# A 3x3 convolution by Winograd rows: the first image pair is loaded in two pieces, one of them ahead of the weights

## The chip, the cores and the metric

The kernel runs on one core of one Trainium2 chip. The metric is the device time of one execution in microseconds, lower is better. Before the change it is 126.67 us, the median of three runs (126.33 to 126.72).

A core has five engines that run side by side and wait for one another by semaphores: TensorE (PE) for matrix products, VectorE (DVE), ScalarE (ACT) and GpSimd (POOL) for elementwise work, and SyncE (SP), which here only issues transfers. Transfers between the chip's main memory and the core's own memory run on 16 DMA engines, which serve the queues of SyncE, ScalarE and GpSimd together.

## The reference

Sixteen images of 64 channels and 64 x 64 pixels are convolved with 128 filters of 64 x 3 x 3, with a border of one zero pixel. All is float32.

```python
x_pad = np.pad(x, ((0, 0), (0, 0), (1, 1), (1, 1)), mode='constant')
output = np.zeros((batch, c_out, h, w), dtype=np.float32)
for b in range(batch):
    for co in range(c_out):
        for ci in range(c_in):
            for kh in range(3):
                for kw in range(3):
                    output[b, co] += weight[co, ci, kh, kw] * x_pad[b, ci, kh:kh+h, kw:kw+w]
```

The input is 16.8 MB and the output 33.6 MB.

## The kernel before

**Tiling.** Two images make a pair: their 2 x 64 channels fill the 128 partitions. There are eight pairs (p = 0 to 7; "pair 1" of the change's description is p = 0). Each output row pair needs three products where the plain method needs more: with G0, G1, G2 the three filter rows, the kernel computes U = G1 times the sum of two neighbouring input rows, A = (G2 - G1) and G0 on shifted rows, B = (G0 - G1) and G2 on shifted rows. The even output rows are A + U, the odd ones B + U. So it needs, for each pair, the input in f16 (`xs`), the sums of neighbouring rows in f16 (`ss`), and the five weight matrices in `Wt`.

**Weights.** SyncE loads them as they lie (`w_raw`, line 42). GpSimd casts them to f16 (line 61). TensorE transposes them by 18 small matmuls with an identity (line 93), ACT copies the result to `Wt` in three pieces (line 94: G1, G2, G0), and GpSimd forms the two differences (lines 96 and 97). These take a stretch at the start in which no other work can be done on TensorE, so `spin(10)` behind the transposes gives it ten matmuls on zeros (line 56), whose results nobody reads.

**The first pair.** SyncE loads it as f32 (`x0`, line 45) behind the weights. DVE makes its sums in four blocks of eight row pairs (line 76), ACT its f16 copy in four casts of 18, 16, 16 and 14 rows (line 101). Pairs p = 1 to 3 also come as f32 from SyncE (`xf`, line 49); their sums are made by GpSimd and their casts by ACT (line 169). Pairs 4 to 7 are loaded by GpSimd's own queue, which converts to f16 on the way (line 67); the first of these, `load(4)`, stands behind the weight differences on GpSimd.

**The loop.** For each pair there are four blocks of 16 output rows; in each, TensorE makes U, A and B (line 150; the channels of the two images lie in different halves of the array, so that matmuls go in twos), ACT copies U out of the accumulators (`ut`, line 164), and DVE adds A + U and B + U (lines 174 and 177) into output tiles. The accumulators are eight banks that go round. Each finished image of a pair is stored in one transfer of 2 MB (two of 1 MB for the last pair): the first image from SyncE, the second from ACT's queue one block later (line 106).

**Order.** `keep` fixes the program order of what it wraps against other such instructions of that engine; each engine then works in that order. Transfers of one queue are served in the order of their issue.

Of the kernel before, what the change touches and what calls it, by code (L numbers as in the profile page):

```python
# [13 lines left out]
def kernel(  # L14
# [6 lines left out]
    nc = tc.nc  # L21
    B, CI, H, W = x.shape
# [3 lines left out]
    RB = 8  # L26

    keep = tc.keep_in_program_order
    x_rows = x.rearrange("b c h w -> (b c) h w")
    out_rows = out.rearrange("b co h w -> b co h w")  # L30
    w_flat = weight.rearrange("co ci kh kw -> co (ci kh kw)")
# [7 lines left out]


    w_raw = const.tile([CO, CI * 9], F32)
    nc.sync.dma_start(w_raw, w_flat)
    x0 = opool.tile([128, H, W], F32, tag="ot", name="x0")
    cuts = [(0, 18), (18, 34), (34, 50), (50, 64)]
    nc.sync.dma_start(x0, x_rows[0:128, :, :])
    xf = {}
    for p in (1, 2, 3):
        xf[p] = opool.tile([128, H, W], F32, tag="ot", name="xf")
# [5 lines left out]
    def spin(n):  # L54
        for _ in range(n):
            keep(nc.tensor.matmul(warm, zeros[:, 0:128], zeros))  # L56
# [6 lines left out]
    xs = {p: xpool.tile([128, H, W], F16, tag="xs", name="xs") for p in range(4)}  # L63

    def load(p):
        xs[p] = xpool.tile([128, H, W], F16, tag="xs", name="xs")
        keep(nc.gpsimd.dma_start(xs[p], x_rows[128 * p : 128 * p + 128, :, :]))  # L67
# [3 lines left out]
    def sums(eng, p, src, lo, n):  # L71
        if p not in ss:
            ss[p] = spool.tile([128, H // 2, W], F16, tag="ss", name="ss")
        v = src.rearrange("p (j i) c -> p j i c", i=2)
        keep(
            eng.tensor_add(  # L76
                ss[p][:, lo : lo + n, :], v[:, lo : lo + n, 0, :], v[:, lo : lo + n, 1, :]
            )
        )
# [5 lines left out]
    def wrow(i):  # L85
        return Wt[:, i, :, :].rearrange("p t c -> p (t c)")

    for kh, g in ((1, G1), (2, G2), (0, G0)):
        wp = psum.tile([128, 512], F32, tag="acc", name="wp")
        for k in range(3):  # L90
            t = 3 * kh + k
            for q in (0, 64):
                keep(nc.tensor.matmul(wp[q : q + 64, k * CO : k * CO + CO], w16[:, t::9], ident))  # L93
        keep(nc.scalar.copy(wrow(g), wp[:, 0 : 3 * CO]))  # L94
    spin(10)
    keep(nc.gpsimd.tensor_sub(wrow(G21), wrow(G2), wrow(G1)))  # L96
    keep(nc.gpsimd.tensor_sub(wrow(G01), wrow(G0), wrow(G1)))  # L97
    load(4)
    for n, (lo, hi) in enumerate(cuts):
        sums(nc.vector, 0, x0, RB * n, RB)  # L100
        keep(nc.scalar.copy(xs[0][:, lo:hi, :], x0[:, lo:hi, :]))  # L101

    held = []
# [7 lines left out]
    for p in range(NP):  # L111
# [8 lines left out]
        for blk in range(4):  # L120
# [58 lines left out]
            if blk in parts:  # L179
                lo, hi = parts[blk]  # L180
# [34 lines left out]
```

## Time and profile before

| what | value |
|---|---|
| median of three runs | 126.67 us (126.33 to 126.72) |
| span of the profiled execution | 124.8 us, so about 1.9 us of the median lie around the span |
| busy: PE, DVE, ACT, POOL | 108.2, 82.8, 52.0, 36.2 us |
| moved by the DMA engines | 46.57 MB, mean 373 GB/s |
| read from and written to main memory | 17.07 MB and 33.55 MB, 406 GB/s over the span |
| weights: issued, cast by GpSimd starts | 0.74 us, 3.59 us |
| x0: issued, first sum and first cast start | 1.17 us, 8.80 us |
| ten spins | 5.55 us, for 4.44 us |
| first matmul of line 150 | 9.92 us |
| last matmul ends, last DVE sum ends | 111.4 us, 113.9 us |

The profile is one execution; times count from the start of its span. "Busy" is time in which an engine works on an instruction; issuing a transfer is not counted. In the view of groups a line gives the source line, engine, operation and tiles, then busy time, mean duration and the idle time ahead with what ended it. The chain of work that ended last is followed back from the last instruction to whatever released it. The view by stretches gives, for each stretch of the span, the busy time (and number of instructions) of PE, the weight loads of PE, DVE, ACT and POOL, the clock granted to TensorE, the mean busy share of the 16 DMA engines, and the rate at which they moved data. That share can pass 1 in a short stretch, as a transfer's time is put down where it is recorded.

### The profile page before, as it was taken

The page shows a single profiled execution, that of the slowest core. Times are in us where ns is not written, and L with a number is a line of the kernel's source. Part 1 is how long each engine was busy: PE and PEld are TensorE (multiplying, and loading weights), DVE is VectorE, ACT ScalarE, POOL GpSimd, SP SyncE. Part 2 cuts the span into 40 slices and gives each one's busy share as a digit, 9 for nine tenths or more (in the row PEclk, how much of TensorE's full clock was granted, in tenths as well). Part 3 has the DMA queues.
Part 4 walks back from the last instruction along what each step waited for, and adds up shares of the span by engine and source line. Part 5 has one row for each costly group of instructions (what it writes and reads, how often), then busy time and mean ns, then how long its engine had stood idle before and what let it go on. Part 6 is the DMA issues. An engine that isn't in the chain of part 4 may idle for free.

```text
span 124.8 us, 2437 instructions
## 1 busy us (share of the span) xinstructions
PE 108.2 (87%) x988; PEld 49.3 (40%) x988; DVE 82.8 (66%) x133; ACT 52.0 (42%) x84; POOL 36.2 (29%) x27
## 2 busy tenths in 40 slices
PE   0699999999999999999999999999999999990000
PEld 0433444444444444444444444444444444440000
DVE  0016787878878787877777778777877787685000
ACT  4319749833993399333333333333333333330000
POOL 2360086294799202920067000940000000000000
PEclk9999999999999999999999999999999999999555
DMA  6899999999999999999999999999999999999991
GB/s 173 362 436 407 297 323 349 425 315 415 397 349 368 305 376 373 360 334 362 381 347 360 334 344 412 431 431 425 425 441 420 436 415 425 436 412 418 436 402 74
DMA packets 3898, 46.57 MB, mean 373 GB/s; under 512 B 432, under 2 KB 432, under 8 KB 560
## 3 DMA queue, kind: packets, MB, share of 16 engines
q1 hardware_dynamic: 2016, 25.46, 49.5%
q10 hardware_dynamic: 1296, 16.78, 31.6%
q0 software_dynamic: 576, 4.19, 16.1%
q8 instruction: 7, 0.11, 0.3%
q14 instruction: 3, 0.02, 0.0%
HBM read 17.07 MB, written 33.55 MB: 406 GB/s over the span
## 4 chain that ended last, share of the span: by engine, by line
PE 86%; DMA 2%; DVE 1%; issue 1%; POOL 1%; DVEq 0%
PE acc L150 81%; PE warm L56 4%; DMA w_raw<-in_weight_dram 2%; PE wp L93 1%; DVE ot L174 1%; POOL w L61 1%; DVE ot L177 0%; DVEq L210 0%; DVEq L174 0%
## 5 line engine op out<-in xcount | busy, mean ns | idle before, releaser
L150 PE MATMUL acc<-xs,Wt 64*128 64x504 f16 (+3 forms) x768 | 87.0, 373 | 0.0
L150 PEld LDWEIGHTS <-Wt 64*128 64x128 f16 x960 | 46.8, 94 | 56.2 <-issue 0.8
L164 ACT COPY ut<-acc 128x512 f32<-128x512 f32 x64 | 34.3, 588 | 52.9 <-issue 32.1
L174 DVE TENSOR_TENSOR ot<-acc,ut 128x512 f32<-128x512 f32 x64 | 41.2, 686 | 22.6 <-PE acc L150 18.3
L177 DVE TENSOR_TENSOR ot<-acc,ut 128x512 f32<-128x512 f32 x64 | 41.1, 684 | 0.0
L150 PE MATMUL acc<-ss,Wt 64*128 64x504 f16 (+1 forms) x192 | 26.0, 377 | 0.0
L76 POOL TENSOR_TENSOR ss<-xs 128x1024 f16<-128x1024 f16 x8 | 16.8, 2124 | 20.2 <-DMA xs<-in_x_dram 20.2
L76 POOL TENSOR_TENSOR ss<-xf 128x1024 f16<-128x1024 f32 x6 | 14.1, 2361 | 13.6 <-DMA xf<-in_x_dram 13.6
L169 ACT CAST xs<-xf 128x1024 f16<-128x1024 f32 x12 | 12.0, 1058 | 0.0
L76 DVE TENSOR_TENSOR ss<-x 128x512 f16<-128x512 f32 x4 | 2.5, 687 | 7.7 <-DMA x<-in_x_dram 7.7
L93 PE MATMUL wp<-ident,w 128*64 128x128 f16 x18 | 1.3, 328 | 4.3 <-POOL w L61 4.3
L101 ACT CAST xs<-x 128x1024 f16<-128x1024 f32 (+2 forms) x4 | 3.9, 1042 | 2.6 <-DMA x<-in_x_dram 2.6
L67 POOL DMA_DIRECT2D xs<-in_x_dram x4 | 2.4, 600 | 7.8 <-ACT xs L169 7.8
L56 PE MATMUL warm<-zeros 128*128 128x512 f16 x10 | 4.4, 631 | 0.0
L93 PEld LDWEIGHTS <-w 128*64 128x64 f16 x18 | 1.1, 210 | 4.3 <-POOL w L61 4.3
L94 ACT CAST Wt<-wp 128x384 f16<-128x384 f32 x3 | 1.2, 487 | 2.9 <-PE wp L93 2.9
L56 PEld LDWEIGHTS <-zeros 128*128 128x128 f16 x10 | 1.3, 143 | 2.3 <-issue 2.2
L94 ACT ACT_TABLE_LOAD x1 | 1.3, 1283 | 0.7 <-PEq L199 0.7
L96 POOL TENSOR_TENSOR Wt<-Wt 128x384 f16<-128x384 f16 x1 | 0.9, 907 | 1.7 <-ACT Wt L94 1.7
L61 POOL CAST w<-w_raw 128x576 f16<-128x576 f32 x1 | 0.7, 663 | 2.3 <-DMA w_raw<-in_weight_dram 2.3
L97 POOL TENSOR_TENSOR Wt<-Wt 128x384 f16<-128x384 f16 x1 | 0.9, 910 | 0.0
L51 DVE MEMSET zeros<- 128x256 uint32 x1 | 0.3, 272 | 0.9 <-PEq L199 0.9
(6 smaller groups left out, 0.9 us busy)
## 6 DMA issues: line engine op xcount, KB each, us to landing
out_dram<-ot SPq DMA_DIRECT2D x7, 2048.0 KB, 22.0
out_dram<-ot ACTq DMA_DIRECT2D x7, 2048.0 KB, 18.9
xf<-in_x_dram SPq DMA_DIRECT2D x3, 2048.0 KB, 22.1
xs<-in_x_dram POOLq DMA_DIRECT2D x4, 1024.0 KB, 23.4
x<-in_x_dram SPq DMA_DIRECT2D x1, 2048.0 KB, 7.6
out_dram<-ot SPq DMA_DIRECT2D x2, 1024.0 KB, 10.6
out_dram<-ot ACTq DMA_DIRECT2D x2, 1024.0 KB, 11.0
w_raw<-in_weight_dram SPq DMA_DIRECT2D x1, 288.0 KB, 2.8
```

The source lines that it names most:

```text
L56: keep(nc.tensor.matmul(warm, zeros[:, 0:128], zeros))
L61: keep(nc.gpsimd.tensor_copy(w16, w_raw))
L67: keep(nc.gpsimd.dma_start(xs[p], x_rows[128 * p : 128 * p + 128, :, :]))
L76: eng.tensor_add(ss[p][:, lo : lo + n, :], v[:, lo : lo + n, 0, :], v[:, lo : lo + n, 1, :])
L93: keep(nc.tensor.matmul(wp[q : q + 64, k * CO : k * CO + CO], w16[:, t::9], ident))
L94: keep(nc.scalar.copy(wrow(g), wp[:, 0 : 3 * CO]))
L101: keep(nc.scalar.copy(xs[0][:, lo:hi, :], x0[:, lo:hi, :]))
L150: nc.tensor.matmul(tiles[b2][:, lo - j0 : hi - j0, c_lo:c_hi], Wt[p0 : p0 + 64, wi, kw, :], rhs, start=i == 0, stop=i == n - 1,)
L164: keep(nc.scalar.copy(ut, U[b2]))
L169: keep(nc.scalar.copy(xs[q][:, lo : lo + 16, :], xf[q][:, lo : lo + 16, :]))
L174: nc.vector.tensor_add(ots[b2][:, j0 : j0 + RB, 0, :], A[b2], us[b2])
L177: nc.vector.tensor_add(ots[b2][:, j0 : j0 + RB, 1, :], Bt[b2], us[b2])
```

## The change

SyncE now issues x0 in two transfers, rows 0 to 31 of every channel ahead of the weights and rows 32 to 63 behind them. The first two blocks of sums and the first cast (18 rows), which need only rows 0 to 31, stand ahead of the weights' work in program order, and the loop that did all four now does the rest. Of the filler matmuls, nine stand ahead of the transposes and two behind them, in place of ten behind. Lines of the changed kernel are six higher in the loop (150 becomes 156, 164 becomes 170, 174 and 177 become 180 and 183).

```diff
     w_raw = const.tile([CO, CI * 9], F32)
-    nc.sync.dma_start(w_raw, w_flat)
     x0 = opool.tile([128, H, W], F32, tag="ot", name="x0")
     cuts = [(0, 18), (18, 34), (34, 50), (50, 64)]
-    nc.sync.dma_start(x0, x_rows[0:128, :, :])
+    keep(nc.sync.dma_start(x0[:, 0:32, :], x_rows[0:128, 0:32, :]))
+    keep(nc.sync.dma_start(w_raw, w_flat))
+    keep(nc.sync.dma_start(x0[:, 32:H, :], x_rows[0:128, 32:H, :]))
...
+    spin(9)
+    sums(nc.vector, 0, x0, 0, RB)
+    sums(nc.vector, 0, x0, RB, RB)
+    keep(nc.scalar.copy(xs[0][:, 0:18, :], x0[:, 0:18, :]))
     for kh, g in ((1, G1), (2, G2), (0, G0)):
...
-    spin(10)
+    spin(2)
     keep(nc.gpsimd.tensor_sub(wrow(G21), wrow(G2), wrow(G1)))
     keep(nc.gpsimd.tensor_sub(wrow(G01), wrow(G0), wrow(G1)))
     load(4)
-    for n, (lo, hi) in enumerate(cuts):
-        sums(nc.vector, 0, x0, RB * n, RB)
+    for n, (lo, hi) in enumerate(cuts[1:]):
+        if n:
+            sums(nc.vector, 0, x0, RB * (n + 1), RB)
         keep(nc.scalar.copy(xs[0][:, lo:hi, :], x0[:, lo:hi, :]))
```

## Prediction

> **What bounds the kernel now.** I read first the chain of work that ended last. It names TensorE almost alone, and it puts the weights' arrival and the filler matmuls at its head:
>
> ```profile
> 0.74 2.79 DMA w_raw<-in_weight_dram
> 3.59 0.67 POOL w L61
> 4.30 1.31 PE wp L93 x16
> 5.62 4.37 PE warm L56 x10
> 9.99 101.39 PE acc L150 x948
> ...
> 113.32 0.60 DVE ot L177
> ```
>
> Read alone, this says that every microsecond by which line 150 starts earlier is a microsecond off the end. But the chain stops at 113.9 us and the span is 124.8, so I next read the busy time by stretches; the last two columns are the mean busy share of the 16 DMA engines and what they moved (GB/s):
>
> ```profile
> 0.00:3.00 3.00, 0.00 (x0) 0.00 (x0) 0.27 (x1) 1.28 (x1) 0.70 (x6) 1.00 0.61 174
> 3.00:6.00 3.00, 1.70 (x20) 1.30 (x21) 0.00 (x0) 1.04 (x3) 0.76 (x2) 1.00 0.86 350
> 6.00:10.00 4.00, 4.00 (x12) 1.24 (x12) 1.20 (x2) 1.41 (x3) 2.33 (x3) 1.00 1.03 442
> 10.00:26.00 16.00, 16.00 (x152) 7.37 (x154) 12.30 (x21) 11.73 (x17) 6.39 (x3) 1.00 1.03 363
> 26.00:29.00 3.00, 3.00 (x32) 1.34 (x28) 2.27 (x5) 1.07 (x2) 3.00 (x3) 1.00 0.89 273
> 29.00:80.00 51.00, 51.00 (x482) 23.33 (x480) 39.85 (x65) 24.73 (x40) 20.57 (x12) 1.00 1.02 366
> 80.00:99.00 19.00, 19.00 (x180) 8.64 (x178) 14.79 (x25) 6.44 (x12) 2.50 (x2) 1.00 1.00 428
> 99.00:105.00 6.00, 6.00 (x60) 2.83 (x58) 4.69 (x9) 2.15 (x4) 0.00 (x0) 1.00 1.02 431
> 105.00:114.00 9.00, 7.55 (x72) 3.23 (x66) 7.44 (x12) 2.15 (x4) 0.00 (x0) 1.00 0.99 419
> 114.00:120.00 6.00, 0.00 (x0) 0.00 (x0) 0.00 (x0) 0.00 (x0) 0.00 (x0) 0.64 1.01 429
> ```
>
> The DMA engines are full from 6 us to 120 us, apart from 26 to 29. From 80 us on, while TensorE still works, they move 428 to 431 GB/s, no less than at 114 to 120 when nothing else runs. The 363 and 366 are no slack: the GpSimd loads read f32 and are counted by the f16 that they write (4.19 MB for twice that read). The issues by line confirm a queue:
>
> ```profile
> out_dram<-ot SPq DMA_DIRECT2D x7, 2048.0 KB, 22.0
> out_dram<-ot SPq DMA_DIRECT2D x2, 1024.0 KB, 10.6
> x<-in_x_dram SPq DMA_DIRECT2D x1, 2048.0 KB, 7.6
> w_raw<-in_weight_dram SPq DMA_DIRECT2D x1, 288.0 KB, 2.8
> ```
>
> A 2 MB store needs about 5 us at 430 GB/s and lands after 22; the last 1 MB stores need 2.4 us and land after 10.6. So the transfers set the end: they start at about 1.7 us and run without a hole until the last store.
>
> **How much cover that gives.** The narrowest place is the store of pair 7 (p=6): SyncE issues its first half at 100.54 us, and the stores of the pair before, issued at 87.7 and 88.3, land 15.6 us later, at about 103.3. From an issue to its first traffic takes 1.0 us (weights issued at 0.74, traffic from 1.7), so new work is there at 101.6. The 16 engines do not run dry all at once, some by about 101.6 and the last at 103.3. I take 1.0 us of cover there, with ends 0.5 and 1.7. At the last stores (issued 113.3 and 114.0, landing about 10 us later, against 4.9 us for 2 MB plus the 2.05 us of fixed time worked out below) it is about 3 us.
>
> **The sum's base.** The profiled execution is a span of 124.8 us; the median of three runs is 126.67, so 1.9 us lie around the span. I add the change to 126.67.
>
> **The change part by part.** *SyncE's issues.* There are three before the xf loads in place of two, at 0.42 us each, so the xf issues move back 0.4 us. They queue behind 2.4 MB of earlier transfers (until 8.8 us) and are not waited for: 0. If that cover were gone, 0.4.
>
> *Arrivals.* Weights: 2.79 us from issue to landing. x0's 2 MB come 5.27 us later (8.80 against 3.53), 398 GB/s, so 1 MB is 2.63 us and the weights 0.74, which leaves 2.05 fixed. After the change: first half at 0.74 + 2.05 + 2.63 = 5.4, weights at 6.2 (2.6 later), second half at 8.8 as now. Smaller pieces of 8 KB a row cost nothing by the row of 114 to 120, where only the last stores' pieces of that size are moving much of the time, at 429.
>
> *Weights' work.* It moves as a block behind 6.2: GpSimd's cast to 6.9, the 18 transposing matmuls from 6.96 and the two spins from 8.2; at 0.444 us a spin (4.44 for 10) line 150's work starts at 9.1 instead of 9.92: 0.8 us earlier. Its inputs: ACT's copy of G1 by 8.1; G21, ending 2.5 us after the transposes start as now (6.82 - 4.30), at 9.5, needed after the first six matmuls at 9.8; G01 at 10.3, needed at 11.1. The first two blocks of sums (0.69 us each) and the short cast (1.15) stand on DVE and ACT between 5.4 and 6.8, when both are idle: 0, and the ACT copies of the weights queued behind that cast are not due before 7.6. If the half came 1.5 us late, those copies and all behind them would be.
>
> *What is late next.* The three remaining casts on ACT run from 8.8 for 1.04 + 1.04 + 0.93 to 11.8; the copies ut behind them start there instead of at 12.59. They free the first accumulators, which the second block's next group wants at about 13.1 on the faster course, so nothing is lost. Pair 2's sums end at 20.88 and are needed at 22.74 - 0.8 = 21.9: covered by 1.0.
>
> *GpSimd's queue.* load(4) stands behind the weight subtractions and is issued at 10.3 instead of 7.63. Its data are first read at 37.07 and landed after about 22: 0. The xf loads meanwhile have the engines to themselves; the bytes are the same.
>
> *The nine early spins.* They wait only for the zeros (1.13 us) and take until 5.1; then TensorE idles until 7.0. The 10 spins of before ran at 0.444 us each, while in line 150's work 24 matmuls take 2.68, two side by side, so 0.22 a pair: every spin was at half speed and the full rate came at about 9.9, 5.6 us after TensorE's first matmul at 4.30 (the clock column says 1.00 throughout and does not show this). With the early spins forgotten in the gap, 5.6 us after 6.96 is 12.6; real work from 9.1 to 12.6 at half speed loses 1.75 us, so TensorE ends 0.9 later than now. With the early spins counted, the filler goes at 0.22 and work starts at 8.7 at full rate, 1.2 earlier. Ends for TensorE's finish: -1.2 and +0.9; I take the middle, about -0.1, as the gap lies between the two rows. For the end of the kernel all but the late end is covered by the full queue: 0, with ends of -1.2 (if the queue does not decide) and +0.4 (0.9 less 0.5 of cover).
>
> The Trainium skill, "TensorE: Matmul & The Clock Gate", section "What's actually happening", says that the array runs at half rate until one busy window of about 3.4 us, and that these windows run free of the kernel. By that rule full rate could come as late as two windows after 6.96, an estimate of 13.8, and TensorE would end up to 1.5 us late, the kernel 0.5 us late beside the 1.0 of cover; by the row of 5.6 us it is 0. The trace agrees that a start is at half rate for longer than one such window (5.6 us).
>
> *The DMA start.* Here the change can really move the end. Single microseconds of the same view:
>
> ```profile
> 2.00:3.00 1.00, 0.00 (x0) 0.00 (x0) 0.00 (x0) 0.02 (x1) 0.00 (x0) 1.00 1.62 478
> 3.00:4.00 1.00, 0.00 (x0) 0.00 (x0) 0.00 (x0) 0.00 (x0) 0.41 (x1) 1.00 0.70 248
> 4.00:5.00 1.00, 0.69 (x12) 0.70 (x14) 0.00 (x0) 0.04 (x1) 0.25 (x1) 1.00 0.88 377
> ```
>
> At the turn from weights to x0 the rate falls to 248 and 377 where 430 is usual: (182 + 53)/430 = 0.55 us lost. If the turn is the cause, a large first piece in front could hide it: -0.55. If it is the first touch of x, it only moves to the front, and a second turn is added: +0.1 or so. I take -0.1, near the latter, as the loss sits in x0's first transfers.
>
> **Sum:** 126.67 - 0.1 + 0 = 126.6 us. I treat 0.3% (0.4 us) as what a measurement of this kernel can tell from no change; the three runs of before spread over 0.39.
>
> **The rivals.** (1) *TensorE decides.* For it: the chain view, 86% TensorE. Against it: the full DMA engines to 120 us. If true, the end follows the start of line 150, -1.2: 125.5. Chance 0.10.
>
> (2) *The transfers lose less.* The hole at 26 to 29 us is 3 x (430 - 273)/430 = 1.1 us, and 0.55 at the start. Part of either can go, since stores and load(4) meet the xf loads at other moments: half the hole and some of the start, -0.7: 126.0. For it: nothing but the order of transfers differs there, and the order changes. Against it: the same reads and the same first stores remain. Chance 0.17.
>
> (3) *Slower: the array stays at half speed.* Place: line 150's first 24 or so matmuls, after the gap from 5.1 to 7.0. Price: +0.9 for TensorE, less 0.5 of cover at 101.6: +0.4, 127.1. It decides once TensorE is late by more than the cover (0.5 to 1.7). For it: all ten spins of before at half speed, and the gap. Against it: the cover. Chance 0.13.
>
> (4) *Slower: the hole grows.* One more like that at 26 to 29, in part: +0.7, 127.4. For it: it is unexplained. Against it: it is there once in 120 us. Chance 0.07.
>
> **How the numbers follow.** My case, the transfers decide and lose about as much as now, has 0.53: 126.6, own range 126.3 to 127.0. Faster by over 0.3%: (1) and (2), 0.27. Within: 0.53. Slower: (3) and (4), 0.20. The range 125.8 to 127.5 leaves out case (1), some of (2) and the upper part of (4), 0.18 in all.
>
> **What would show it.** Right: line 150 starts at 8.7 to 9.2 and the DMA share stays near 1.0 from 6 to 120 us, so that the distance between DVE's last sum and the span's end grows by whatever TensorE gained. The first matmuls at 0.22 or 0.44 us a pair tell (3). The rates at 2 to 5 and 26 to 29 tell (2) and (4). I am wrong if DMA share falls below 0.95 around 100 to 103 us, or if the end moves one for one with line 150's start.

## The result and the profile after

The changed kernel takes 127.14 us (median of 21 runs, 126.47 to 128.48) against 126.71 us of the kernel before in the same series. The ratio is 1.0039, 95% interval [1.0022, 1.0055]: slower, by 0.3 to 0.7 us, where no change (126.6) was forecast. Two of the 21 runs, 128.38 and 128.48, were slow executions and are not in the ratio. In the profiled execution the span is 125.2 us against 124.8.

The chain of work that ended last, changed kernel (start us, duration us, what):

```profile
1.16 5.95 DMA w_raw<-in_weight_dram
7.17 1.08 POOL w L62
8.29 1.31 PE wp L98 x18
9.59 0.97 PE warm L57 x2
10.56 102.58 PE acc L156 x948
...
115.08 0.60 DVE ot L183
```

Against the kernel before, the weights are 3.6 us later at GpSimd (7.17, 3.59), line 156's work begins at 10.56 in place of 9.99, and it takes 102.58 us in place of 101.39. TensorE's last matmul therefore ends at 113.14, 1.76 us later than before (111.38).

The busy time by stretches, changed kernel (the last two columns are the DMA engines' mean busy share and GB/s):

```profile
0.00:3.00 3.00, 1.81 (x5) 0.70 (x6) 0.27 (x1) 1.28 (x1) 0.70 (x6) 1.00 0.51 101
3.00:6.00 3.00, 2.21 (x6) 0.46 (x4) 0.00 (x0) 0.00 (x0) 0.00 (x0) 1.00 0.93 369
26.00:29.00 3.00, 3.00 (x32) 1.65 (x30) 2.40 (x5) 0.90 (x2) 1.60 (x2) 1.00 1.01 423
29.00:80.00 51.00, 51.00 (x482) 27.71 (x480) 39.84 (x65) 24.51 (x41) 21.63 (x12) 1.00 1.02 360
99.00:105.00 6.00, 6.00 (x61) 3.32 (x58) 4.68 (x9) 2.15 (x4) 0.00 (x0) 1.00 0.86 360
```

The stretch to look at is 99 to 105 us: 0.86 and 360 GB/s, where the kernel before had 1.02 and 431. That is about 0.14 x 6 = 0.84 us in which the DMA engines had nothing to do, although TensorE was busy throughout. With each packet counted over the time that it runs, and not where it is recorded, it is 0.7 us: all 16 engines have a packet at 101.2, eleven at 102.0, five at 103.0 and all again at 103.4. In the kernel before all 16 have one throughout. The stores of p=6 were issued at 102.30 and 102.90 (100.54 and 101.14 before), and the stores ahead of them had run out. Two smaller differences: the first 6 us move 1.41 MB instead of 1.57, and the dip at 26 to 29 us (273 GB/s before) is gone, while 29 to 80 us runs at 360 instead of 366 GB/s.

The start in order of time, changed kernel, shows where TensorE's 1.76 us come from (start, busy time, engine, line, operation, count, and in brackets the idle time ahead):

```profile
6.42 1.29 DVE L77 TENSOR_TENSOR ss<-x 128x512 f16<-128x512 f32 x2 [5.29 <-DMA x<-in_x_dram]
7.17 1.07 POOL L62 CAST w<-w_raw 128x576 f16<-128x576 f32 x1 [5.86 <-DMA w_raw<-in_weight_dram]
8.29 1.31 PE L98 MATMUL wp<-ident,w 128*64 128x128 f16 x18 [3.08 <-POOL w L62]
9.53 1.03 PE L57 MATMUL warm<-zeros 128*128 128x512 f16 x2
10.49 1.46 PE L156 MATMUL acc<-ss,Wt 64*128 64x512 f16 x6
11.74 3.27 PE L156 MATMUL acc<-xs,Wt 64*128 64x512 f16 x24
```

The same groups of matmuls in the kernel before:

```profile
9.92 0.82 PE L150 MATMUL acc<-ss,Wt 64*128 64x512 f16 x6
10.58 2.68 PE L150 MATMUL acc<-xs,Wt 64*128 64x512 f16 x24
```

The first piece of x0 is there at 6.42, the weights at 7.1; GpSimd's cast, running beside VectorE's sums, takes 1.07 us instead of 0.66; and the first groups of line 156 take 1.46 and 3.27 us where the same groups took 0.82 and 2.68 before, 1.23 us more, because TensorE was still at half speed.

### The profile page after: what moved, and what is told of

Its sections match the earlier page's. It is cut to its first block, busy times and chain, and to the rows that moved or that the text cites. A ratio compares the mean times of both kernels' runs of the same rounds, so it can differ in the third digit from the quotient of the medians.

```text
span 125.2 us, 2441 instructions
## 1 busy us (share of the span) xinstructions
PE 110.1 (88%) x989; PEld 57.8 (46%) x989; DVE 83.7 (67%) x133; ACT 52.0 (42%) x84; POOL 37.3 (30%) x27
## 4 chain that ended last, share of the span: by engine, by line
PE 84%; DMA 5%; DVE 1%; POOL 1%; issue 1%; DVEq 0%; SPq 0%
PE acc L156 82%; DMA w_raw<-in_weight_dram 5%; PE wp L98 1%; POOL w L62 1%; PE warm L57 1%; DVE ot L180 1%; DVEq L216 0%; DVE ot L183 0%; SPq L44 0%; DVEq L180 0%
## 5 line engine op out<-in xcount | busy, mean ns | idle before, releaser
L156 PE MATMUL acc<-xs,Wt 64*128 64x504 f16 (+3 forms) x768 | 88.1, 375 | 0.0
L156 PEld LDWEIGHTS <-Wt 64*128 64x128 f16 x960 | 55.4, 95 | 48.8 <-issue 1.3
L156 PE MATMUL acc<-ss,Wt 64*128 64x504 f16 (+1 forms) x192 | 27.2, 384 | 0.0
L77 DVE TENSOR_TENSOR ss<-x 128x512 f16<-128x512 f32 x4 | 3.3, 867 | 7.1 <-DMA x<-in_x_dram 7.1
L57 PE MATMUL warm<-zeros 128*128 128x512 f16 x11 | 5.1, 627 | 1.2 <-DVE zeros L52 1.2
L92 ACT CAST xs<-x 128x1152 f16<-128x1152 f32 x1 | 1.2, 1152 | 4.4 <-DMA x<-in_x_dram 4.4
L107 ACT CAST xs<-x 128x1024 f16<-128x1024 f32 (+1 forms) x3 | 2.9, 1031 | 0.0
L101 POOL TENSOR_TENSOR Wt<-Wt 128x384 f16<-128x384 f16 x1 | 1.1, 1145 | 1.6 <-ACT Wt L99 1.6
L102 POOL TENSOR_TENSOR Wt<-Wt 128x384 f16<-128x384 f16 x1 | 1.4, 1357 | 0.0
```

Of the source, the lines that this page charges most:

```text
L77: eng.tensor_add(ss[p][:, lo : lo + n, :], v[:, lo : lo + n, 0, :], v[:, lo : lo + n, 1, :])
L92: keep(nc.scalar.copy(xs[0][:, 0:18, :], x0[:, 0:18, :]))
L156: nc.tensor.matmul(tiles[b2][:, lo - j0 : hi - j0, c_lo:c_hi], Wt[p0 : p0 + 64, wi, kw, :], rhs, start=i == 0, stop=i == n - 1,)
```

## The experiments

The theory formed from these two traces, called the hole theory: the transfers set the end; TensorE's start may move freely as long as the store of p=6 is issued before the DMA engines run dry at about 102 us; the changed kernel makes TensorE 1.76 us late and so crosses that point. The rival, called the order theory: loading x0 in two pieces, one ahead of the weights, costs transfer time by itself. A third, TensorE decides the end, as the chain view says.

Every profile is of one execution, while the ratios are of 6 to 21 runs. The profiled execution is not always a typical one: with 18 early fillers it took 127.10 us against a median of 126.69, and with the split alone 127.72 against 126.62, both without a hole. So positions and shares below hold for one execution each, and the hole is not all that makes executions of one kernel differ.

### More filler, so that TensorE is not late

```diff
-    spin(9)
+    spin(18)
```

> The changed kernel with 18 filler matmuls ahead of the transposes in place of 9, so that TensorE does not idle before the weights arrive. The hole theory (the changed kernel is slower because TensorE, 1.8 us late, issues the store of pair p=6 so late that the DMA engines run dry at about 102 us): full rate comes by about 8 us, line 156's work runs at 0.22 us a pair from the start, TensorE's last matmul ends at 111.4 to 112 instead of 113.1, the DMA share at 99 to 105 us returns from 0.86 to about 1.0, and the time falls to that of the kernel before, 126.6 to 126.8, ratio 1.000 +- 0.002. The order theory (the two-piece load and the new order at the start cost DMA time by themselves): the first microseconds of transfers are unchanged, the time stays at about 127.1, ratio 1.004.

Measured: 126.69 us, ratio 1.000 [0.9974, 1.0027]. The chain of this run, its last part, and the stretch:

```profile
10.68 100.91 PE acc L156 x942
```

```profile
99.00:105.00 6.00, 6.00 (x60) 3.34 (x58) 4.86 (x8) 2.15 (x4) 0.00 (x0) 1.00 1.01 426
```

The loads are those of the changed kernel; the last matmul ends at 111.59, the hole is gone, and the ratio is back at 1.000, although the two intervals still overlap a little (1.0022 to 1.0027). What the longer filler changes is the gap: TensorE idles only 0.16 us ahead of the transposes, and the trace's clock record has full speed from 6.23 us on, before line 156 starts.

### The stores of p=6 in halves

```diff
-            parts = {3: (0, 64)} if p < NP - 1 else {1: (0, 32), 3: (32, 64)}
+            parts = {3: (0, 64)} if p < NP - 2 else {1: (0, 32), 3: (32, 64)}
```

This was done to the changed kernel, to the kernel before, and to the kernel before with 18 fillers in place of 10.

> The changed kernel, start untouched, but the two images of pair p=6 are stored in halves (as those of the last pair are), so that 2 MB of stores are issued about 6 us before the place where the DMA engines ran dry. Hole theory: TensorE stays late (last matmul at about 113), the share at 99 to 105 us rises from 0.86 to about 1.0, and the time falls by most of the 0.77 us of empty engine time there, to 126.3 to 126.8, ratio 0.997 to 1.001. Order theory: no change, ratio 1.004.

> The kernel before, with the stores of pair p=6 in halves: the control for the run in which the halves were added to the changed kernel and did not bring it back (ratio 1.006). If the halves themselves cost (288 more pieces of 8 KB, two issues more): ratio 1.003 to 1.006 here too, and the hole theory stands. If they cost nothing (ratio 0.998 to 1.002), then filling the hole at 102 us did not help, and TensorE's lateness costs by another way than the hole.

> The kernel before with 18 fillers and with the halves: TensorE 1.3 us late, as in the run with 18 fillers alone (ratio 1.005, DMA share 0.88 at 99 to 105), but with cover at 102 us. Hole theory: the share there is back at 1.0, and the time is that of the kernel before with halves alone (difference below 0.002). If lateness costs by another way: 0.004 to 0.006 above the halves alone.

Measured: on the changed kernel 1.0060 [1.0019, 1.0101], on the kernel before 1.0036 [1.0003, 1.0068], on the late one 1.0021 [0.9987, 1.0054]. The stretch of the changed kernel with halves, then of the late kernel with halves:

```profile
99.00:105.00 6.00, 6.00 (x60) 3.34 (x58) 4.69 (x9) 2.15 (x4) 0.00 (x0) 1.00 0.99 418
```

```profile
99.00:105.00 6.00, 6.00 (x60) 2.81 (x58) 4.96 (x8) 1.82 (x5) 0.00 (x0) 1.00 0.99 415
```

No hole is left in either, and my expectation for the first run was still missed: the time did not fall. The control, measured on another chip, says why in part: halves cost 0.0036 by themselves. With the halves in place the late kernel is not above the early one, as the hole theory has it, but this is a weak test: in its profile TensorE's last matmul ends at 112.20, only 0.82 us late and not the 1.3 expected. The point estimate of the changed kernel with halves (1.0060), where TensorE is 1.93 us late, stays above the control; the intervals overlap widely. So these runs do not decide between the theories, and that filling the hole brings the time back is not shown by them.

### The kernel before, made late step by step

The filler behind the transposes is raised from 10 to 14, 18 and 26; nothing else is touched.

```diff
-    spin(10)
+    spin(18)
```

> The kernel before, with 18 filler matmuls behind the transposes in place of 10: loads and their order untouched, line 150's work starts 1.7 to 2.4 us later (8 more fillers at 0.22 to 0.44 us). Hole theory: with about 0.7 us of cover at 102 us the time rises by 0.7 to 1.4 us, to 127.4 to 128.0, ratio 1.005 to 1.011, and the share at 99 to 105 us falls to 0.8 to 0.88. Order theory (the end does not hang on TensorE by that little): ratio 1.000 to 1.002.

> The kernel before with 14 fillers: work of line 150 starts 0.2 to 1.0 us later than with 10, between the kernel before and the one with 18. Hole theory with a cover of about 0.7 us: ratio 1.000 to 1.003, DMA share at 99 to 105 between 0.94 and 1.0. Cost in proportion to lateness without any cover: 1.003 to 1.006.

> The kernel before with 26 fillers: 8 more than in the run with 18, so TensorE's work starts another 1.7 us (8 x 0.22) later, 3.0 in all. Hole theory: the cover is used up, so every further microsecond is a microsecond of hole: DMA share at 99 to 105 falls from 0.88 to 0.58 to 0.65 and the time rises by 1.7 to about 129.2, ratio 1.018 to 1.021. If the cost of lateness is spread and not a hole: a ratio of 1.008 to 1.012.

With 14 fillers TensorE was not late in the profile, against what was expected (last matmul ends 111.13, as full speed came early there, at 7.65), and the ratio is 1.0018 [0.9991, 1.0044]. With 18 it ends 1.30 us later than in the kernel before, with 26 2.92 us later. The stretch in the two, 18 first:

```profile
99.00:105.00 6.00, 6.00 (x60) 2.84 (x58) 4.69 (x9) 1.81 (x5) 0.00 (x0) 1.00 0.88 369
```

```profile
99.00:105.00 6.00, 6.00 (x60) 2.74 (x58) 4.69 (x8) 2.15 (x4) 0.00 (x0) 1.00 0.75 314
```

Ratios: 1.0050 [1.0016, 1.0085] and 1.0191 [1.0136, 1.0247]. The first is at the lower end of what the hole theory gave, the second in the middle. Here the loads and their order are those of the kernel before, so lateness of TensorE alone makes the hole and the loss. The share with 26 fillers was expected at 0.58 to 0.65 and was 0.75. The hole is 0.25 x 6 = 1.50 us and some 0.27 more behind the stretch (0.97 at 105 to 114 us), while the time rose by 2.4 us: about 0.6 us of it lies outside the hole and was not explained.

### TensorE earlier than in the kernel before

Two kernels, one from either order of loads. In the first, x0 comes in two pieces behind the weights, 4 fillers do, and ACT makes the later casts of x0 inside the loop:

```diff
-    spin(10)
+    spin(4)
...
-        keep(nc.scalar.copy(xs[0][:, lo:hi, :], x0[:, lo:hi, :]))
+        if n == 0:
+            keep(nc.scalar.copy(xs[0][:, lo:hi, :], x0[:, lo:hi, :]))
...
+            for lo, hi in {0: cuts[1:3], 1: cuts[3:]}.get(blk, ()) if p == 0 else ():
+                keep(nc.scalar.copy(xs[0][:, lo:hi, :], x0[:, lo:hi, :]))
```

> The kernel before with x0 in two pieces, both behind the weights, 4 fillers in place of 10, and the casts of x0's rows 18 to 63 moved on ACT behind the copies of the first blocks: line 150's work starts as soon as the first piece is there, and TensorE's last matmul should end at 108.5 to 110, 1.5 to 3 us earlier than before (111.4). Hole theory: the DMA engines are full all the same and nothing is gained, 126.4 to 126.8, ratio 0.998 to 1.001; the last stores are issued earlier and land later. TensorE decides (the chain view): 124 to 125.2, ratio 0.98 to 0.988.

Measured: the last matmul ends at 109.88, 1.50 us earlier than before, and the ratio is 1.0005 [0.9992, 1.0019]. Its chain and its last stores (issues by line, us to landing):

```profile
7.44 102.44 PE acc L152 x948
```

```profile
out_dram<-ot SPq DMA_DIRECT2D x2, 1024.0 KB, 12.6
out_dram<-ot ACTq DMA_DIRECT2D x2, 1024.0 KB, 12.1
```

They land after 12.6 and 12.1 us, where those of the kernel before took 10.6 and 11.0: what TensorE gains is spent waiting in the queue. "TensorE decides" asked for a ratio of 0.98 to 0.988 and is out.

The second is the changed kernel with 18 early fillers and the weights' cast on VectorE ahead of the sums:

```diff
-    keep(nc.gpsimd.tensor_copy(w16, w_raw))
+    keep(nc.vector.tensor_copy(w16, w_raw))
```

> The changed kernel with 18 early fillers and with the weights' cast on VectorE ahead of the first sums, so that GpSimd's cast (1.07 us beside those sums, 0.66 alone in the kernel before) is off the chain: line 156's work starts 0.4 to 0.8 us earlier than with 18 fillers alone, and TensorE's last matmul ends at 110.7 to 111.3, earlier than in the kernel before (111.4). Hole theory: nothing is gained by it, as the DMA engines are full either way: 126.5 to 126.8, ratio 0.998 to 1.001. TensorE decides: 126.0 to 126.3, ratio 0.994 to 0.997.

Measured: last matmul at 110.73, 0.65 us early, no hole (share 1.00), ratio 1.0030 [0.9999, 1.0061]. Nothing is gained, and the point lies above the 1.001 expected: as high as that of a kernel with a hole (1.0029, next section). The hole theory alone does not say why.

### The parts of TensorE's lateness

The nine early fillers are taken out; and, in another kernel that keeps the nine, only the weights' cast goes to VectorE.

```diff
-    spin(9)
```

> The changed kernel without its nine early fillers: TensorE's first matmul is the first transpose at about 8 us. If the nine fillers were forgotten in the gap behind them: full rate comes at 11.5 to 15 as in the changed kernel (12.9 and 13.8 in two profiles), TensorE's last matmul ends at 112.5 to 114 and the time is that of the changed kernel, ratio 1.003 to 1.007. If the nine fillers did bring full rate on: it is later without them, last matmul beyond 114, ratio 1.009 or more.

> The changed kernel, nine early fillers as they are, with only the weights' cast moved to VectorE ahead of the first sums. It takes the 0.4 us of GpSimd's slowing beside VectorE (1.07 against 0.66) and 0.2 more off the chain of the weights, and leaves the late full rate as it is. Expected by the hole theory: transposes at about 7.3 instead of 8.3, TensorE's last matmul at 112 to 113, a hole half as deep, ratio 1.001 to 1.003. If GpSimd's slowing were the main cause: ratio 1.000 or less.

The stretch with the cast on VectorE (without the nine the share is 0.98):

```profile
99.00:105.00 6.00, 6.00 (x61) 3.33 (x58) 4.69 (x8) 2.00 (x4) 0.00 (x0) 1.00 0.87 358
```

Without the nine: 1.0018 [0.9999, 1.0037], last matmul at 112.22. With them (the changed kernel) it was 113.14. Full speed did not come later without them, so in these profiles they bring nothing; the interval overlaps that of the changed kernel, so that they harm is not shown. With the cast on VectorE: 1.0029 [1.0006, 1.0052], last matmul at 112.92, the share at 99 to 105 us 0.87, so the hole is not half as deep, as was expected, but as deep as before. The transposes start at 7.28 instead of 8.29, and yet TensorE gains only 0.2 us, for it works at half speed for longer (its first record of full clock is at 13.54 us). So GpSimd's slowing is a part of the chain; that it does not decide rests on this one execution, which was one of the longer ones (127.33 us against a median of 126.83).

### The order of the loads by itself

x0 alone in two pieces behind the weights, all else as in the kernel before:

```diff
-    nc.sync.dma_start(x0, x_rows[0:128, :, :])
+    keep(nc.sync.dma_start(x0[:, 0:32, :], x_rows[0:128, 0:32, :]))
+    keep(nc.sync.dma_start(x0[:, 32:H, :], x_rows[0:128, 32:H, :]))
```

> The kernel before with x0 loaded in two pieces, both behind the weights: one more issue and one more completion, order of the bytes and all engine work as before. Hole theory: TensorE's work starts at the same time, ratio 1.000 +- 0.002. Order theory, if the splitting is what costs: ratio 1.003 to 1.004; if only the place of the weights costs, 1.000 too.

Measured: 0.9985 [0.9953, 1.0017]. The split costs nothing that shows. For the place of the weights, the early kernel of above (18 fillers, cast on VectorE) was run again beside a twin with the weights first:

```diff
+    keep(nc.sync.dma_start(w_raw, w_flat))
     keep(nc.sync.dma_start(x0[:, 0:32, :], x_rows[0:128, 0:32, :]))
-    keep(nc.sync.dma_start(w_raw, w_flat))
```

> Once more the changed kernel with 18 early fillers and the cast of the weights on VectorE (first piece of x0 ahead of the weights, TensorE early, no hole at 102 us), beside its twin with the weights first. Theory of a second, small cost of the order: x0 first moves 1.41 to 1.51 MB in the first 6 us in six profiles, the weights first 1.50 to 1.62 MB in eight, on the mean 0.27 us of transfers less, so 1.001 to 1.003 here. Theory that the hole is the only cost: 0.999 to 1.001.

> The twin: the same kernel with one exchange among the issues of SyncE, the weights ahead of the first piece of x0. Last matmul of TensorE at 109.5 to 111, no hole. Theory of a second, small cost of the order: 1.5 to 1.62 MB in the first 6 us, ratio 0.999 to 1.001, lower than its twin by 0.002. Hole alone: the same ratio as its twin.

Measured: x0 first 1.0019 [1.0001, 1.0037], weights first 1.0010 [0.9997, 1.0022]. The first 6 us move 1.47 MB with x0 first and 1.54 MB with the weights first (1.41 to 1.51 and 1.50 to 1.62 in the other profiles). Both points lie where a small cost of the order would put them, but the times of the twins are not told apart. The kernels with x0 first and no hole, or next to none, lie at 1.000, 1.0018, 1.0019 and 1.0030, on the mean 1.0017; those with the weights first and no hole at 1.0005, 1.0018, 0.9985 and 1.0010, on the mean about 1.0005. So up to about 0.2% of the 0.39% may be a cost of the order, or of something else that was not found; it is unlikely to be the whole. How much of the changed kernel's own loss the hole makes stays open between about half and all.

No kernel tried beats the kernel before.

## Why the prediction was wrong

**What was right.** The transfers set the end. The profile says so more plainly than the chain does: TensorE's last matmul moved from 1.50 us early to 2.92 us late over the kernels with whole stores of p=6. Up to about 0.8 us of lateness there is next to no hole and the time did not follow TensorE's end, the ratios scatter from 0.9985 to 1.0030; beyond it all four kernels have a hole and an interval clear of 1:

| kernel | last matmul ends, against before | DMA share, 99 to 105 us | ratio and interval |
|---|---|---|---|
| two pieces behind the weights, 4 fillers | -1.50 | 1.01 | 1.0005 [0.9992, 1.0019] |
| weights first, 18 early fillers, cast on VectorE | -0.86 | 0.99 | 1.0010 [0.9997, 1.0022] |
| changed, 18 early fillers, cast on VectorE | -0.65 | 1.00 | 1.0030 [0.9999, 1.0061] |
| the same kernel again | -0.34 | 1.01 | 1.0019 [1.0001, 1.0037] |
| before, 14 fillers | -0.25 | 1.01 | 1.0018 [0.9991, 1.0044] |
| changed, 18 early fillers | +0.21 | 1.01 | 1.000 [0.9974, 1.0027] |
| two pieces behind the weights | +0.42 | 1.00 | 0.9985 [0.9953, 1.0017] |
| changed, no early fillers | +0.84 | 0.98 | 1.0018 [0.9999, 1.0037] |
| before, 18 fillers | +1.30 | 0.88 | 1.0050 [1.0016, 1.0085] |
| changed, cast on VectorE | +1.54 | 0.87 | 1.0029 [1.0006, 1.0052] |
| changed | +1.76 | 0.86 | 1.0039 [1.0022, 1.0055] |
| before, 26 fillers | +2.92 | 0.75 | 1.0191 [1.0136, 1.0247] |

The place (store of p=6, about 102 us) was right, and the cover there (1.0 us, ends 0.5 and 1.7) fits: lateness less empty engine time is 1.30 - 0.72, 1.54 - 0.78, 1.76 - 0.84 and 2.92 - 1.50, which is 0.6 to 1.4 us. The sign that the prediction named for being wrong, a share below 0.95 there, is what came. Rival (3), slower by half speed and a drained queue at that place, is in the main what happened; it had a chance of 0.13. That its time was 127.1 and 127.14 was measured is luck: it took TensorE as 0.9 late and the cover as 0.5, where TensorE was 1.76 late, 0.57 of it from a late start where this rival had an early one, and the cover by the hole was 0.9.

**The step that failed** is the one that sized TensorE's finish: "Ends for TensorE's finish: -1.2 and +0.9; I take the middle, about -0.1". It was +1.76, outside both ends. By its terms:

- *Arrivals.* The first piece was to be there at 5.4 and came at 6.42; the weights were to land at 6.2 and landed at 7.11: +0.9. The fixed 2.05 us and 398 GB/s were taken from the kernel before, where the weights' small transfer is the first to go; with x0 first, the first 3 us move 101 GB/s (174 before). Other profiles with this order have the weights at 6.6 to 7.1, so 0.4 to 0.9.
- *GpSimd's cast.* Taken as 0.66, measured 1.07: +0.4. The step put the sums and the short cast at 0 since "both are idle" and named no neighbour on GpSimd. They ran at the same time as the cast.
- *Half speed.* The late end put full speed at 12.6 and 1.75 us of loss behind a start at 9.1. It came at 12.93 by the trace's clock record, and the loss is 1.23 us, by the two groups shown, since work began later. So this term went as the late end had it, and taking the middle dropped most of it.

Sum: the late end, +0.9, with 1.3 more from arrivals and cast and 0.5 less of half speed, is +1.7. Seen in the chain: line 156's work is 0.57 later (10.56 against 9.99) and 1.2 slower in its first groups. The middle between the two ends was no estimate: the early end needed the nine fillers to count behind a gap of 1.9 us, later in fact 3.1, and the row of 5.6 us from a first matmul already spoke for the late one. Three gaps in one direction add up, and the cover of 1.0 us was only large enough for one or two. When full speed comes differs from one execution to the next (in the profile of the changed kernel with halves, the same program up to p=6, at 13.84 and not 12.93), so 1.76 is the lateness of the profiled execution, not of every one.

**The other terms.** *The DMA start*, -0.1 with ends of -0.55 and +0.1: the first 6 us moved 1.41 MB and not 1.57, 0.16 MB or 0.37 us less at 430 GB/s, so the sign was wrong. What of it reaches the end is open, as said. *SyncE's issue, load(4), ACT's casts, pair 2's sums* at 0: as forecast; load(4) was issued at 12.29 and was not waited for. *Rivals (2) and (4), the dip at 26 to 29 us*: it went from 273 to 423 GB/s, a gain of 1.05 us at that place, but 29 to 80 us fell from 366 to 360 GB/s, 51 x 6/430 = 0.71 us. In the profiles with whole stores it is there (251 to 289) from 0.9 us early to 0.4 late, weaker at 1.5 early and 0.8 late (355, 350), and gone from 1.3 late on (410 to 431). The prediction calls it a hole, but the engines were not empty: counted over the time that packets run, 0.98 of the stretch is taken, and the packets there took 721 ns in the median against 611 in the three microseconds behind it. Why they were slow was not looked for. *Rival (1)* is excluded by the kernel that is 1.50 us early.

The range 125.8 to 127.5 held the time. The sign was missed.

## What to carry to other kernels

Read an engine that the transfers cover as covered on one side only: find the store at which the queue has least in front of it, state the cover there in microseconds, and then ask for every term of the change whether it can make that store later. Such terms add up with their signs: take neither the middle of two ends that come from different mechanisms nor the calm duration of an instruction that the change puts beside another engine's. A filler that ends long before the work it prepares may do nothing: here nine, ending 2.1 to 3.1 us ahead of the transposes, brought nothing in three profiles, while 18, ending at most 1.0 us ahead, had full speed on in time. Whether the number or the gap decides was not tested.

## What was not expected of the hardware

**GpSimd and VectorE slow each other.** GpSimd in order of time, the changed kernel with 18 early fillers and the cast on VectorE:

```profile
8.86 0.92 POOL L101 TENSOR_TENSOR Wt<-Wt 128x384 f16<-128x384 f16 x1 [7.54 <-ACT Wt L99]
9.72 1.36 POOL L102 TENSOR_TENSOR Wt<-Wt 128x384 f16<-128x384 f16 x1
```

Of two subtractions of the same size, the one begun while VectorE was idle takes 0.92 us; the other, begun after VectorE's second pair of sums had started at 9.24, takes 1.36. Those two sums span 2.40 us there, against 1.29 alone, and in the changed kernel the cast beside the sums takes 1.07 against 0.66. The Trainium skill, "SBUF — State Buffer", section "SBUF: two separate sides", says that GpSimd and a VectorE instruction with two inputs from that memory take the same pair of ports by an exclusive lock, so that the later one waits for the whole of the other. The trace agrees in kind, though the size is less: 0.4 us for the cast whose start lies 0.54 us before the sums' end (7.17, and 6.42 + 1.29 = 7.71).

**When full speed comes.** The trace's clock record, whose first entry is full speed (the view by stretches shows 1.00 ahead of it as well), has that entry 2.8 to 6.3 us after TensorE's work last began without a longer break: 4.30 to 9.85 in the kernel before, 8.29 to 12.93 in the changed one, 7.99 to 11.37 without early fillers, 7.28 to 13.54 with the cast on VectorE, and, with 18 early fillers from 1.19 on, 6.23, 4.68, 3.98 and 4.76 in four profiles. The nine early fillers, 4 us of work, left no trace behind the gap. The Trainium skill, "TensorE: Matmul & The Clock Gate", section "What's actually happening", has this as one busy window of about 3.4 us that runs free of the kernel; up to two windows, 6.8 us, is an estimate from that. The longest measured (6.3) fits the estimate; the shortest (2.8) is less than one window, so if there are such windows, these traces say that one need not be busy throughout.

**Smaller stores.** Storing p=6 as four transfers of 1 MB instead of two of 2 MB costs 0.0036 (ratio 1.0036 [1.0003, 1.0068], so barely clear of nothing) with the DMA share at 99 to 105 us at 0.98; why was not tested.
